# Linear attention's queries and keys: the high and the low activations in one 512-column product

## The chip, the cores and the metric

The kernel runs on one core of a Trainium2 chip. The metric is the device time of one execution in microseconds; before the change the median of three runs is 917.91 us (917.15 to 918.28). A core has a matrix engine (TensorE, in the profile PE, with its weight loads as PEld), a vector engine (VectorE, DVE), a scalar engine (ScalarE, ACT), GpSimd (POOL) and SyncE (SP), which issues most of the loads. They run side by side, each with its own queue of instructions in a fixed order, and meet at semaphores. Matrix products are accumulated in PSUM, which the kernel uses as eight banks of 128 partitions x 512 floats.

## The reference

A two-layer encoder trunk for 256 tokens of width 1024, all in float32. Of each layer, this is what the change touches:

```python
u = rms_norm(h, g_mix_pre)
(gq, gk, gv, gg, ra_f, ra_b, aq, ak, av, gate_a, gate_b) = jnp.split(u @ w_in, offsets, axis=-1)
qh = gq.astype(f32).reshape(b, s, GLA_HEADS, GLA_DK) * (GLA_DK ** -0.5)
kh = gk.astype(f32).reshape(b, s, GLA_HEADS, GLA_DK)
```

`gq` and `gk` are the queries and keys of the gated linear attention: 4 heads of 128, so 512 columns each. The other columns of the same product go to the linear attention's values, gates and decays, to the grouped-query attention (8 query heads, 2 key and value heads) and to the two branch gates. After the two branches come their merge, an output projection, a SwiGLU feed-forward part and a per-layer input embedding.

## The kernel before

**Precision in three products.** A matrix product in full float32 precision is put together from products of a faster 32-bit type. Each operand x is split into a high part (a rounding of x) and a low part (x minus the high part), and instead of x·y three products are accumulated: high·high, high·low and low·high. Weights arrive by DMA as raw float32 in units of 512 rows x 512 columns (1 MB); ACT copies a unit to its high part `wh`, DVE subtracts to get the low part `wl` (`split`, L131 to L133), in two pieces of 128x1024. The stream of units (`Stream`) runs ahead of the products by a set depth. Activations are turned by PE, so that the width lies on the partitions, and are split in the same way.

**Where the split activations lie.** `Split` (L404) keeps them in tiles of four blocks of 128 rows: `t[p, k, s, t]`, with k the block, s = 0 for high and 1 for low, and t the token (256). The high and the low part of one block of rows are therefore 512 neighbouring floats on each partition.

**The stage that is changed.** Most of the input projection uses the activations as the stationary operand and streams 512 columns of weights (`amode`). The linear attention's queries and keys are wanted turned, with the head's width on the partitions, so there the weights are stationary and the 256 tokens stream past (`wmode`, L630, called by `project_t`, L729). `project_t` works through two units of weights (halves of the 1024 rows); in each, for each of four column blocks f of 128 (a head), it issues for four blocks of rows k the products wh·high and wh·low, and after those wl·high: twelve products of 256 columns. Two heads share one bank, so a projection holds two banks. The stage at L1269 to L1280 calls it for the queries and then for the keys and empties each bank with one ACT copy of 128x512, the queries scaled by 128 to the power -0.5.

**What sets the order around it.** The program writes down the products of one stage after the other; side jobs (`Task`) are woken by a count of steps (`tick`, one per column block in `wmode`) and put their instructions between. During this stage these are the turning of the grouped-query attention's queries (L1240) and keys (L1178, split at L1180 by way of L133), its scores (L1199 by way of L105), the softmax (L1201 to L1219) and the turning of its result (L1227); right after it the linear attention's decays begin (L1296 and following), which first read the stored queries and keys in L1323 and L1324. A planner then fixes each engine's order ahead of the run from its own estimate of durations and from priorities (the order of writing, moved ahead in places), and gives out the PSUM banks. At run time each engine follows its list.

Of the kernel before, what the change touches and what calls it, by code (L numbers as in the profile page):

```python
# [13 lines left out]
AF = mybir.ActivationFunctionType  # L14
ALU = mybir.AluOpType
AX = mybir.AxisListType

P = 128
T = 256
# [40 lines left out]
def trunk_kernel(ctx: ExitStack, tc: tile.TileContext, a: dict, out: bass.AP):  # L60
# [7 lines left out]
    nc = tc.nc  # L68
# [13 lines left out]
    def nm(s):  # L82
        uid[0] += 1
        return f"{s}_{part[0]}_{uid[0]}"

    def big(dt=F32):
        return bigp.tile([P, 2048], dt, tag="big", name=nm("big"))
# [4 lines left out]
    def acc():  # L92
        return accp.tile([P, 512], F32, tag="acc", name=nm("acc"))

    def aux():
        return accp.tile([P, 512], F32, tag="acc", name=nm("aux"))

    def t512():
        return smp.tile([P, 512], F32, tag="t512", name=nm("t512"), bufs=5)
# [4 lines left out]
    def mm(o, lhsT, rhs, start, stop):  # L104
        return nc.tensor.matmul(o, lhsT, rhs, start=start, stop=stop)  # L105
# [7 lines left out]
    def passes(o, parts, start, stop, fresh=False, between=None, **kw):  # L113

        ps = [((xh, yh), (xh, yl), (xl, yh)) if fresh else ((xh, yh), (xl, yh), (xh, yl)) for (xh, xl), (yh, yl) in parts]
        seq = [p for t in ps for p in t[:2]] + [t[2] for t in ps]
        for n, (x, y) in enumerate(seq):  # L120
            nc.tensor.matmul(o, x, y, start=start and n == 0, stop=stop and n == len(seq) - 1, **kw)  # L121
            if between is not None and 2 * (n + 1) == len(seq):
                between()

    def vmul(out, in0, in1):
        nc.vector.tensor_tensor(out=out, in0=in0, in1=in1, op=ALU.mult)
# [9 lines left out]
    h = cp.tile([P, 2, D], F32, tag="h", name="h")  # L136
# [30 lines left out]
    def unit(w, kh, c0):  # L167

        return lambda t: [
            (  # L170
                t[:, :2048].rearrange("p (k c) -> p k c", c=512),
                w[kh * 512 : (kh + 1) * 512, c0 : c0 + 512].rearrange("(k p) c -> p k c", p=P),
            )
        ]
# [29 lines left out]
    for l in range(DEPTH):  # L204
# [6 lines left out]
        pair = [unit(w, kh, C_GB + j * 512) for kh in range(2) for j in range(2)]  # L211
# [12 lines left out]
        for x in FFN.replace("p", ""):  # L224
            if x == "1":
                pair = pairs.pop(0)
# [170 lines left out]
    def tick():  # L397

        for t in list(tasks):
            t.left -= 1  # L400
            if t.left <= 0:
                t.go()

    class Split:  # L404
# [33 lines left out]
        def all(self, k):  # L438
            return [t[:, 0, :] for t in self.at(k, 1, 0, T)]

    def transpose_in(sp, src, k, n, hf, plain=None):

        ps = aux()
        for i in range(n):
            nc.tensor.transpose(ps[:, i * P : (i + 1) * P], src[:, i * P : (i + 1) * P], ident)
        with tc.high_priority(AHEAD):
            sp.put(ps[:, : n * P], k, n, hf * P, P)
        if plain is not None:
            nc.scalar.copy(plain, ps[:, : n * P])
# [68 lines left out]
    def turn_in(sp, x, hf, wait, plain=None, apart=False):  # L518


        def turn():
            yield wait
            for j, y in enumerate(halves(x)):
                if j and apart:
                    yield 1
                transpose_in(sp, y, 4 * j, 4, hf, plain and plain[j])

        sp.makers[hf].append(Task(turn(), part[0]))
# [100 lines left out]

    def wmode(os_, sp, k0, w, first, last):  # L630

        wh, wl = (t[:, :2048].rearrange("p (k c) -> p k c", c=512) for t in w)
        for hf in range(2):
            sp.need(hf, k0)
        for f in range(4):  # L640
            o = os_[f // 2][:, (f % 2) * T : (f % 2 + 1) * T]
            s = slice(f * P, (f + 1) * P)
            parts = [((wh[:, k, s], wl[:, k, s]), sp.all(k0 + k)) for k in range(4)]
            passes(o, parts, first and f % 2 == 0, last and f % 2 == 1, True)
            tick()

    def times(o, act, first=True, then=None):
# [38 lines left out]
    def seven(sp, forms, gated, alone=()):  # L686

        made, task = forms
        quad = lambda hf, j: lambda k: sp.tok(4 * j + k, hf)
        form = lambda i: lambda k: [p[:, k, :] for p in made[i]]  # L690

        def add(out, x, y):
            nc.vector.tensor_tensor(out=out, in0=x, in1=y, op=ALU.add)

        (p1, v), (p3, p7) = (halves(mid()) for _ in range(2))
        c11, p5, o = acc(), acc(), []
        c12, c22 = p3, p7

        def product(i, then):

            o[:] = [acc()]
            times(o[0], form(i), True, then)

        def both():
            add(v, o[0], v)
            add(c12, v, p3)
            add(c22, v, p7)

        def last():
            vsub(v, p5, c22)  # L710
            gated(1, v, c22)

        times(c11, quad(0, 0), True, lambda: nc.scalar.copy(p1, c11))
        yield
        task.need()
        product(0, lambda: nc.scalar.copy(p3, o[0]))
        yield
        times(p5, form(1), True, lambda: vsub(v, p5, p1))
        yield
        product(2, lambda: nc.scalar.copy(p7, o[0]))  # L720
        yield
        product(3, both)
        yield
        times(c11, quad(0, 1), False, lambda: gated(0, c11, c12))
        yield
        times(p5, (lambda k: [x[:, k * P : (k + 1) * P] for x in alone]) if alone else quad(1, 1), False, last)
        yield

    def project_t(sp):  # L729

        o = [acc(), acc()]
        for kh in range(2):
            wmode(o, sp, kh * 4, ws.take(), kh == 0, kh == 1)
            ws.done()
        return o

    def project(sp):

        o = [acc(), acc()]
        for kh in range(2):  # L740
            w = ws.take()
            for hf in range(2):
                amode(o[hf], sp, hf, kh * 4, w, kh == 0, kh == 1)
            ws.done()
        return o
# [80 lines left out]
    uT = Split()  # L826
# [195 lines left out]
    for l in range(DEPTH):  # L1022
# [109 lines left out]
        o = {}  # L1132
# [137 lines left out]
        ws.depth = 3  # L1270
        qk = big().rearrange("p (x h t) -> p x h t", x=2, t=T)
        for x in range(2):
            o = project_t(uT)
            for i in range(2):
                dst = qk[:, x, 2 * i : 2 * i + 2, :]
                src = o[i].rearrange("p (h t) -> p h t", t=T)
                if x == 0:
                    nc.scalar.activation(dst, src, AF.Copy, bias=0.0, scale=P**-0.5)
                else:
                    nc.scalar.copy(dst, src)  # L1280


        part[0] = f"{l}gla"
# [137 lines left out]
        for j in range(2):  # L1421
            o = project(uT)
            for hf in range(2):
                dst = gg[:, hf, j * 512 : (j + 1) * 512]
# [67 lines left out]
        def merge(br):  # L1492
            def then(j, hf, o):
                sl = [s[:, hf, j * 512 : (j + 1) * 512] for s in sgate[: br + 1]]
                vmul(sl[br], o, sl[br])
                if br == 1:
                    nc.vector.tensor_tensor(out=sl[0], in0=sl[0], in1=sl[1], op=ALU.add)

                    def turn():
                        yield WAIT_MIX[hf]  # L1500
                        transpose_in(mixT, sl[0], 4 * j, 4, hf)

                    mixT.makers[hf].append(Task(turn(), part[0], j))

            return then
# [44 lines left out]
        def turned(src, k, n, hf, wait=WAIT_FFN):  # L1550


            def turn():
                yield wait
                transpose_in(hid, src, k, n, hf)

            hid.makers[hf].append(Task(turn(), part[0], k // 4))

        for hf in range(2):
            ws.lend = hf == 1  # L1560
            for b in range(2):
                o = acc()
# [42 lines left out]
        def pair(b):  # L1605
            def gated(hf, gate, up):
                sg = t512()
                nc.scalar.activation(sg, gate, AF.Silu)
                vmul(sg, up, sg)
                turned(sg, 2 * b, 4, hf, WAIT_LAST[hf] if b == PAIRS[-1] else WAIT_PAIR)  # L1610

            return seven(u2, forms, gated)

        o = []
# [96 lines left out]
        uT = nxt  # L1711
# [47 lines left out]
```

## Time and profile before

| | |
|---|---|
| median of three runs | 917.91 us (917.15 to 918.28) |
| the profiled execution | 916.88 us, span of its instructions 914.8 us |
| busy share of the span | PE 99%, PEld 85%, DVE 86%, ACT 64%, POOL 11% |
| queries' and keys' projections, layer 0 | 41.4 to 70.1 us |
| queries' and keys' projections, layer 1 | 498.7 to 527.5 us |
| mean granted clock of TensorE | 0.997 of full speed |

How to read the rows that follow. In a row of the timeline stand the start in microseconds from the span's beginning, the time from the first start to the last end, the engine, the line of the kernel, the operation, the tile written, an arrow, the tiles read, the shape and the number of instructions in a row; square brackets give idle time before it and who ended it. Matmuls are pipelined, so the duration of a row of them is longer than the distance to the next row's start, and the distance is what they cost. In rows of a tile, `min/median/max` are durations of one instruction in nanoseconds. In the table by stretch, each engine has its busy time in microseconds and the number of its instructions.

### The profile page before, as it was taken

Reading aid. Unit: us, or ns where it says so; the run is one execution under the profiler, and the core shown is the slowest. Engines: PE = TensorE matmul, PEld = TensorE weight load, DVE = VectorE, ACT = ScalarE, POOL = GpSimd, SP = SyncE. Lnnn points to the kernel's source line nnn. Section 1 sums busy time; section 2 is a strip of 40 time slices with the busy share of each in tenths; the row PEclk is TensorE's granted clock in tenths of the full one; section 3 lists DMA queues with packets and bytes.
Section 4 is the critical chain, followed back from the end, with each engine's and each line's share of the span. In section 5 each row is a group of like instructions: output and inputs, shape, how many; then the busy total and the mean of one; then the engine's idle time right before and its main releaser. Section 6 shows DMA issues by size and latency. Waiting matters only on the chain.

```text
span 914.8 us, 12463 instructions
## 1 busy us (share of the span) xinstructions
PE 906.7 (99%) x4679; PEld 776.8 (85%) x4679; DVE 786.3 (86%) x1009; ACT 583.9 (64%) x971; POOL 99.9 (11%) x157
## 2 busy tenths in 40 slices
PE   9999999999999999999999999999999999999996
PEld 8998888888888888888899988888888888888886
DVE  7889989987679998999779789899876899989984
ACT  6688767465567565666676687675644766565563
POOL 3700220400100000000324001110001000000001
PEclk9999999999999999999999999999999999999998
DMA  8663445667385555657566424455573846555361
GB/s 285 213 201 121 139 140 189 214 186 255 123 297 182 197 191 205 228 169 262 176 249 231 138 92 139 138 184 184 196 253 123 277 164 215 219 172 222 134 234 47
DMA packets 89513, 173.47 MB, mean 190 GB/s; under 512 B 3486, under 2 KB 27558, under 8 KB 88940
## 3 DMA queue, kind: packets, MB, share of 16 engines
q1 hardware_dynamic: 89292, 172.53, 55.5%
q8 instruction: 37, 0.61, 0.3%
q14 instruction: 24, 0.20, 0.1%
q10 hardware_dynamic: 160, 0.14, 0.0%
HBM read 169.50 MB, written 3.15 MB: 189 GB/s over the span
## 4 chain that ended last, share of the span: by engine, by line
PE 95%; ACT 1%; DVE 1%; DMA 1%; issue 1%; POOL 0%; POOLq 0%
PE acc_1ffnin L121 12%; PE acc_0ffnin L121 12%; PE acc_1gate L121 7%; PE acc_0gate L121 7%; PE acc_1ffnin L105 7%; PE acc_0ffnin L105 7%; PE acc_0gqk L121 3%; PE acc_1gqk L121 3%; PE acc_0wout L121 2%; PE acc_1wout L121 2%; PE acc_1gg L121 2%; PE acc_0gg L121 2%; PE acc_1v L121 2%; PE acc_0v L121 2%; PE acc_1merge L121 2%; PE acc_0merge L121 2%
## 5 line engine op out<-in xcount | busy, mean ns | idle before, releaser
L133 ACT CAST wh_1ffnin<-raw_1ffnin 128x1024 fp32r<-128x1024 f32 x38 | 38.5, 1048 | 25.9 <-PE acc_1ffnin L105 10.2
L133 ACT CAST wh_0ffnin<-raw_0ffnin 128x1024 fp32r<-128x1024 f32 x38 | 38.2, 1048 | 25.1 <-PE acc_0ffnin L105 9.3
L133 DVE TENSOR_TENSOR wl_1ffnin<-raw_1ffnin,wh_1ffnin 128x1024 fp32r<-128x1024 f32 x38 | 45.0, 1221 | 7.6 <-ACT wh_1ffnin L133 7.4
L133 DVE TENSOR_TENSOR wl_0ffnin<-raw_0ffnin,wh_0ffnin 128x1024 fp32r<-128x1024 f32 x38 | 44.7, 1220 | 7.2 <-ACT wh_0ffnin L133 7.2
L105 PE MATMUL acc_1ffnin<-wh_1ffnin,big_1ffnin 128*128 128x512 f32 x176 | 45.1, 390 | 0.0
L105 PE MATMUL acc_0ffnin<-wh_0ffnin,big_0ffnin 128*128 128x512 f32 x176 | 45.1, 390 | 0.0
L121 PE MATMUL acc_1ffnin<-wh_1ffnin,big_1wout 128*128 128x512 f32 x168 | 42.5, 393 | 0.0
L121 PE MATMUL acc_0ffnin<-wh_0ffnin,big_0wout 128*128 128x512 f32 x168 | 42.5, 393 | 0.0
L105 PEld LDWEIGHTS acc_1ffnin<-wh_1ffnin,big_1ffnin 128*128 128x128 f32 x176 | 33.0, 188 | 6.9
L105 PEld LDWEIGHTS acc_0ffnin<-wh_0ffnin,big_0ffnin 128*128 128x128 f32 x176 | 33.0, 188 | 6.9
L133 DVE TENSOR_TENSOR wl_0ffnin<-lent_0ffnin,wh_0ffnin 128x1024 fp32r<-128x1024 f32 x30 | 35.8, 1218 | 2.2 <-ACT wh_0ffnin L133 2.2
L133 DVE TENSOR_TENSOR wl_1ffnin<-lent_1ffnin,wh_1ffnin 128x1024 fp32r<-128x1024 f32 x30 | 35.8, 1218 | 1.9 <-ACT wh_1ffnin L133 1.9
L121 PEld LDWEIGHTS acc_1ffnin<-wh_1ffnin,big_1wout 128*128 128x128 f32 x168 | 31.1, 188 | 6.2
L121 PEld LDWEIGHTS acc_0ffnin<-wh_0ffnin,big_0wout 128*128 128x128 f32 x168 | 31.1, 188 | 6.2
L133 ACT CAST wh_0ffnin<-lent_0ffnin 128x1024 fp32r<-128x1024 f32 x30 | 30.7, 1052 | 8.2 <-PE acc_0ffnin L105 3.9
L133 ACT CAST wh_1ffnin<-lent_1ffnin 128x1024 fp32r<-128x1024 f32 x30 | 30.7, 1052 | 7.5 <-PE acc_1ffnin L105 3.9
L133 ACT CAST wh_0gate<-raw_0gate 128x1024 fp32r<-128x1024 f32 x20 | 20.0, 1049 | 15.6 <-DMA raw_0gate<-in_w_o_attn_dram 6.5
L133 DVE TENSOR_TENSOR wl_0gate<-raw_0gate,wh_0gate 128x1024 fp32r<-128x1024 f32 x20 | 24.0, 1244 | 6.5 <-ACT wh_0gate L133 6.4
L133 ACT CAST wh_1gate<-raw_1gate 128x1024 fp32r<-128x1024 f32 x20 | 19.9, 1048 | 14.1 <-DMA raw_1gate<-in_w_o_attn_dram 6.3
L133 DVE TENSOR_TENSOR wl_1gate<-raw_1gate,wh_1gate 128x1024 fp32r<-128x1024 f32 x20 | 23.5, 1221 | 5.4 <-ACT wh_1gate L133 5.3
L105 PE MATMUL acc_0ffnin<-wl_0ffnin,big_0ffnin 128*128 128x512 f32 x88 | 24.6, 394 | 0.0
L105 PE MATMUL acc_1ffnin<-wl_1ffnin,big_1ffnin 128*128 128x512 f32 x88 | 24.6, 394 | 0.0
(724 smaller groups left out, 2711.3 us busy)
## 6 DMA issues: line engine op xcount, KB each, us to landing
raw_0ffnin<-in_w_ffn_out_dram SPq DMA_DIRECT2D x11, 1024.0 KB, 5.9
raw_1ffnin<-in_w_ffn_out_dram SPq DMA_DIRECT2D x11, 1024.0 KB, 5.4
lent_0ffnin<-in_w_ffn_in_dram SPq DMA_DIRECT2D x6, 1024.0 KB, 7.5
lent_1ffnin<-in_w_ffn_in_dram SPq DMA_DIRECT2D x6, 1024.0 KB, 7.8
raw_0v<-in_w_in_dram SPq DMA_DIRECT2D x4, 1024.0 KB, 5.1
raw_0gate<-in_w_o_gla_dram SPq DMA_DIRECT2D x4, 1024.0 KB, 5.9
raw_0gate<-in_w_o_attn_dram SPq DMA_DIRECT2D x4, 1024.0 KB, 5.2
raw_0wout<-in_w_ffn_in_dram SPq DMA_DIRECT2D x8, 512.0 KB, 4.7
```

Of the source, the lines that this page charges most:

```text
L105: return nc.tensor.matmul(o, lhsT, rhs, start=start, stop=stop)
L121: nc.tensor.matmul(o, x, y, start=start and n == 0, stop=stop and n == len(seq) - 1, **kw)
L133: return nc.scalar.copy(hi, src), nc.vector.tensor_tensor(out=lo, in0=src, in1=hi.bitcast(F32), op=ALU.subtract)
```

## The change

`wmode` gets four banks instead of two, one for each column block. For each block of rows the stationary high weights meet high and low activations in one product of 512 columns: the high tokens' result lands in the first half of the bank and the low tokens' in the second half. The products with the low weights stay 256 columns wide and are added onto the first half. So eight products of 256 columns become four of 512, and four of 256 stay. The sum of the two halves is made when a bank is emptied: ACT copies the first half (scaled, for the queries) to the stored queries or keys, and DVE reads the second half, scales it and adds it to them. The number of steps that wake side jobs is the same.

```diff
+        def pair(self, k):
+            return self.t[k // 4][:, k % 4, :, :]
...
         wh, wl = (t[:, :2048].rearrange("p (k c) -> p k c", c=512) for t in w)
         for hf in range(2):
             sp.need(hf, k0)
-        for f in range(4):
-            o = os_[f // 2][:, (f % 2) * T : (f % 2 + 1) * T]
+        for f, o in enumerate(os_):
             s = slice(f * P, (f + 1) * P)
-            parts = [((wh[:, k, s], wl[:, k, s]), sp.all(k0 + k)) for k in range(4)]
-            passes(o, parts, first and f % 2 == 0, last and f % 2 == 1, True)
+            for k in range(4):
+                mm(o, wh[:, k, s], sp.pair(k0 + k), first and k == 0, False)
+            for k in range(4):
+                mm(o[:, 0:T], wl[:, k, s], sp.all(k0 + k)[0], False, last and k == 3)
             tick()
...
     def project_t(sp):
 
-        o = [acc(), acc()]
+        o = [acc() for _ in range(4)]
...
         for x in range(2):
-            o = project_t(uT)
-            for i in range(2):
-                dst = qk[:, x, 2 * i : 2 * i + 2, :]
-                src = o[i].rearrange("p (h t) -> p h t", t=T)
-                if x == 0:
-                    nc.scalar.activation(dst, src, AF.Copy, bias=0.0, scale=P**-0.5)
-                else:
-                    nc.scalar.copy(dst, src)
+            for i, o in enumerate(project_t(uT)):
+                dst, r = qk[:, x, i, :], 1.0 if x else P**-0.5
+                nc.scalar.activation(dst, o[:, 0:T], AF.Copy, bias=0.0, scale=r)
+                nc.vector.scalar_tensor_tensor(out=dst, in0=o[:, T:], scalar=r, in1=dst, op0=ALU.mult, op1=ALU.add)
```

## The prediction

> **What bounds the kernel.** First the page's shares, then the chain that ended last, then who waited for whom on PE.
>
> ```profile
> span 914.8 us, 12463 instructions
> PE 906.7 (99%) x4679; PEld 776.8 (85%) x4679; DVE 786.3 (86%) x1009; ACT 583.9 (64%) x971; POOL 99.9 (11%) x157
> PE 95%; ACT 1%; DVE 1%; DMA 1%; issue 1%; POOL 0%; POOLq 0%
> ```
> ```profile
> engine line waited for: us in total, times, longest us
> PE warm L105 <- POOL seed L142: 1.0, 1, 1.0
> PE acc_1rq L121 <- DVE big_0ple L133: 0.2, 1, 0.2
> ```
>
> PE is busy for 99% of the span, makes up 95% of the last chain, and the list of its waits has 1.2 us in it. So the kernel is a queue of matmuls: what leaves PE's queue comes off the end, as long as nothing else makes PE wait. DVE at 86% has little room as a mean, so I look at it in the stretches that the change touches: layer 0's two query and key products, what follows them, and the same two in layer 1.
>
> ```profile
> core 0: us, PE busy (x) PEld busy (x) DVE busy (x) ACT busy (x) POOL busy (x), PEclk, DMA share, GB/s
> 41.40:54.40 13.00, 13.00 (x111) 12.96 (x111) 10.98 (x18) 10.78 (x25) 3.67 (x5) 1.00 0.61 190
> 54.40:70.10 15.70, 15.70 (x134) 15.70 (x133) 14.03 (x30) 12.76 (x28) 0.00 (x0) 1.00 0.72 242
> 70.10:92.00 21.90, 21.90 (x111) 18.45 (x110) 20.01 (x31) 18.80 (x40) 0.00 (x0) 1.00 0.30 99
> 498.70:513.20 14.50, 14.50 (x122) 14.35 (x121) 11.35 (x23) 7.98 (x16) 1.40 (x3) 1.00 0.72 245
> 513.20:527.50 14.30, 14.30 (x122) 14.30 (x122) 10.54 (x22) 10.84 (x26) 0.00 (x0) 1.00 0.27 79
> ```
>
> PE has no gap in any of the five. The granted clock is 1.00. DVE is free for 2.0, 1.7, 1.9, 3.1 and 3.8 us.
>
> **Matmuls: what goes.** The groups that write acc_0gqk, and who empties it (layer 1 has the same counts):
>
> ```profile
> L121 PE MATMUL acc_0gqk<-big_start,wh_0rq x64: 277/283/364, 41.5 to 53.9; 128*128 128x256 f32 x64
> L121 PE MATMUL acc_0gqk<-big_start,wl_0rq x32: 280/283/286, 42.4 to 54.4; 128*128 128x256 f32 x32
> L1278 ACT ACTIVATE big_0gqk<-acc_0gqk x2: 599/600/600, 50.9 to 54.7; 128x512 f32<-128x512 f32 x2
> L1280 ACT COPY big_0gqk<-acc_0gqk x2: 585/596/607, 68.1 to 69.8; 128x512 f32<-128x512 f32 x2
> ```
>
> Per projection 64 products with the high weights wh and 32 with the low ones wl, all 256 columns wide. With four projections (queries and keys, two layers) the 256 wh products become 128 of 512 columns; the 128 wl products stay as they are. The durations above overlap one another (pipelining), so a product's price is the distance from start to start:
>
> ```profile
> 37.83 1.07 PE L121 MATMUL acc_0kv<-wl_0rq,big_start 128*128 128x512 f32 x4
> 38.74 1.98 PE L121 MATMUL acc_0kv<-wh_0rq,big_start 128*128 128x512 f32 x8
> 40.56 1.07 PE L121 MATMUL acc_0kv<-wl_0rq,big_start 128*128 128x512 f32 x4
> 41.46 1.12 PE L121 MATMUL acc_0gqk<-big_start,wh_0rq 128*128 128x256 f32 x8
> 42.41 0.64 PE L121 MATMUL acc_0gqk<-big_start,wl_0rq 128*128 128x256 f32 x4
> 42.90 1.12 PE L121 MATMUL acc_0gqk<-big_start,wh_0rq 128*128 128x256 f32 x8
> ```
>
> Sixteen products of 512 columns take 41.46 - 37.83 = 3.63 us, 226.9 ns each; twelve of 256 take 42.90 - 41.46 = 1.44 us, 120.0 ns each. The columns streamed are the same before and after; what goes is a fixed share per product. One merge saves 2 x 120.0 - 226.9 = 13.1 ns, and 128 merges save **1.68 us**. The weight load that goes with each is inside these distances. Activations are long there: the same ones serve the earlier products from 37.83 on, so asking for high and low at once adds no wait.
>
> **Emptying: what is added.** Eight ACT copies of 128x512 become sixteen of 128x256, and sixteen DVE operations are new: each reads the other half from the bank and adds it to ACT's result. The nearest rows, each with 128x256 from PSUM:
>
> ```profile
> 46.98 0.48 DVE L469 SCALAR_TENSOR_TENSOR big_0kv<-acc_0kv,rs_start,big_0kv 128x256 fp32r<-128x256 f32 x1
> 35.95 0.42 DVE L126 TENSOR_TENSOR mid_0rq<-acc_0rq,rope_start 128x256 f32<-128x256 f32 x1
> 47.84 0.48 ACT L468 ACTIVATE big_0kv<-acc_0kv,rs_start 128x256 fp32r<-128x256 f32 x1
> 50.32 0.37 ACT L133 CAST big_0kv<-aux_0kv 128x256 fp32r<-128x256 f32 x1
> ```
>
> DVE gains 16 x 0.42 to 0.48 = 6.7 to 7.7 us; I take 0.48, since that row is the same operation: 1.9 us per projection. ACT goes from 8 x 0.60 = 4.8 to 16 x 0.37 to 0.48 = 5.9 to 7.7 us; I take 0.48, since it is the scaled form: 0.7 us more per projection. Behind a new DVE operation, which waits for its ACT copy (a pair is 0.48 + 0.48 = 0.96 us, where one copy of 0.60 stood), DVE has weight splits queued, and PE waits for those only when they come late.
>
> None of it is on PE's path if the gaps take it. They nearly do: 1.9 us fits the first stretch (2.0 free) and both of layer 1; the second is 0.2 us over (1.7 free) and spills into the idle time right behind it:
>
> ```profile
> 69.81 1.28 DVE L133 TENSOR_TENSOR mid_0at<-aux_0at,mid_0at 128x512 fp32r<-128x512 f32 x2
> 72.98 1.29 DVE L1303 SCALAR_TENSOR_TENSOR mid_0gla<-aux_0gla,mid_0gla 128x512 f32<-128x512 f32 x2 [1.89 <-ACT mid_0gla L1302]
> 78.22 0.68 DVE L126 TENSOR_TENSOR t_0gla<-big_0gqk,t_0gla 128x512 f32<-128x512 f32 x1
> 58.50 2.36 DVE L133 TENSOR_TENSOR wl_0gqk<-raw_0kv,wh_0gqk 128x1024 fp32r<-128x1024 f32 x2
> 70.10 2.00 PE L121 MATMUL acc_0v<-wh_0gqk,big_start 128*128 128x512 f32 x8
> ```
>
> The queries and keys are first read at 78.22, 8.5 us after the last product, so their longer way costs nothing. Weights are split far ahead: the unit done at 58.50 + 2.36 = 60.86 is used at 70.10, 9 us later, so a split pushed back by 1.9 us is still in time, and so is the next load that takes its raw buffer. Without that cover the whole 7.7 us of DVE would come on top: the far end for this term. No row excludes a small gain either, since the order of instructions is drawn up anew: the lower end is the 0.2 us wait of the list and two more like it, 0.6 us less. I take 0, with the rows of margin as the reason.
>
> **Banks.** A projection now holds four PSUM banks of eight where it held two. The fullest moment is in layer 0:
>
> ```profile
> 58.59 1.12 PE L121 MATMUL acc_0gqk<-big_start,wh_0kv 128*128 128x256 f32 x8
> 60.03 1.60 PE L105 MATMUL aux_0at<-big_0kv,mid_0at 128*128 128x256 f32 x12
> 60.38 0.56 ACT L1210 ACTIVATE mid_0at<-aux_0at,mx_0at,qss_0rq 128x256 f32<-128x256 f32 x1
> ```
>
> At 60.03 the keys' third block of columns is done (three banks), two banks of scores are being read by the exponentials until 60.94, and two new ones begin: seven. It fits, by one; I take 0.
>
> **Sum.** The profiled execution took 916.88 us around its span of 914.8, 1.03 us under the median of 917.91. 916.88 - 1.68 = 915.2 for such an execution, and 917.91 - 1.68 = **916.2** for the median: 0.18% less. Runs of before range over 917.15 to 918.28, so I take 0.2% (1.84 us) as what can be told from no change. The sum lies just inside it, and about half of its outcomes go beyond.
>
> **Rivals.**
> 1. **PE waits for the attention's keys (slower).** The scores stand right behind a DVE split of the turned keys, in the very stretches that get new DVE work:
>
> ```profile
> 53.26 2.36 DVE L133 TENSOR_TENSOR wl_0kv<-raw_0rq,wh_0kv 128x1024 fp32r<-128x1024 f32 x2 [0.53 <-ACT wh_0kv L133]
> 55.54 0.42 DVE L133 TENSOR_TENSOR big_0kv<-aux_0kv,big_0kv 128x256 fp32r<-128x256 f32 x1
> 56.19 1.36 PE L105 MATMUL aux_0at<-big_0kv,mid_0at 128*128 128x256 f32 x10
> 510.04 0.41 DVE L133 TENSOR_TENSOR big_1kv<-aux_1kv,big_1kv 128x256 fp32r<-128x256 f32 x1
> 510.21 1.77 PE L105 MATMUL aux_1at<-big_1kv,mid_1at 128*128 128x256 f32 x12
> ```
>
> Layer 0's split ends at 55.96 and PE goes on with the scores at 56.19: 0.23 us of margin. In layer 1 there is none (PE starts at 510.21, the split ends at 510.45). If the planned order puts the new operations ahead of these splits and PE's order isn't moved with them, PE stands for up to 1.9 us per layer: 917.91 - 1.68 + 3.8 = 920.0. It decides from 0.84 us per layer, two operations of 0.48. Against it: in layer 0 PE already does products between the first scores and these, so the order can give way. Chance 0.20.
> 2. **A bank comes too late.** An eviction stuck behind a pair of splits (2.36 us, as at 53.26) holds a bank that PE needs, where seven of eight are in use. Once per layer: 917.91 - 1.68 + 2 x 2.36 = 921.0. Against it: three of four banks are needed 1.4 us and more after the one before. Chance 0.06.
> 3. **The fixed share isn't saved.** If a product into two halves of a bank costs as much as two products, 2 x 120.0, the PE term is 0: 917.9, no change. The rows above speak against it, since 512 columns at 226.9 ns already fill a whole bank. The Trainium skill (TensorE: Matmul & The Clock Gate, section "Wait — 56ns, not 53.3ns?") has a fixed cost of only about 2.5 ns per warm matmul, measured on bf16. By that figure 128 merges would give an estimated 0.3 us; this trace's f32 products show 13.1 ns and disagree with it. Chance 0.04.
> 4. **A little more than the sum.** The new order also loses PE's small waits, 0.6 us: 917.91 - 1.68 - 0.6 = 915.6. Nothing in the change aims at them. Chance 0.12.
>
> **Chances.** The sum has the remaining 0.58; half goes beyond 0.2% (0.29), half stays within (0.29). Faster: 0.29 + 0.12 = 0.41. Same: 0.29 + 0.04 = 0.33. Slower: 0.20 + 0.06 = 0.26. The likeliest case alone holds 915.4 to 917.0 (the runs' spread around it). The range over all cases reaches from 915.0 (rival 4 and the same spread) to 920.0, rival 1's full price; rival 2 and half of rival 1's outcomes beyond are left out.
>
> **What would show it.** Right: 128 products of 512 columns at about 227 ns write acc_0gqk and acc_1gqk, 64 each, beside 64 each of 256 at 120; a layer's two projections take 0.84 us less; PE's list of waits stays near 1.2 us; sixteen DVE rows of about 0.48 us and sixteen ACT rows of 0.4 to 0.5 read the banks. Wrong: a wait of PE on big_0kv or big_1kv (rival 1), on a DVE operation that reads acc_0gqk or acc_1gqk (rival 2), or products at 240 ns (rival 3).

## The result and the profile after

The changed kernel takes 915.57 us (median of 22 runs, 914.70 to 917.20) against 917.40 us before (22 runs, 916.21 to 919.63): a ratio of 0.998 with a 95% interval of 0.9973 to 0.9986, so 1.8 us faster, 1.3 to 2.5 by the interval. In a later set of runs it is 915.48 against 917.10, a ratio of 0.9981 (0.9972 to 0.9990).

The page of the changed kernel's first profiled execution: its span, the engines' busy times with the number of instructions, and the DMA queue q8 (packets, MB, share), which matters below.

```profile
span 915.2 us, 12243 instructions
PE 905.9 (99%) x4551; PEld 769.6 (84%) x4551; DVE 791.1 (86%) x1025; ACT 584.5 (64%) x979; POOL 103.0 (11%) x157
...
q8 instruction: 36, 0.59, 0.3%
```

PE has 128 products fewer, DVE 16 operations and ACT 8 more: the change as written. The span is 0.4 us longer than before's, although the median is shorter. This execution took 917.14 us, at the slow end of its runs, and the list of PE's waits shows where most of that lies:

```profile
engine line waited for: us in total, times, longest us
PE warm L105 <- POOL seed L142: 1.0, 1, 1.0
PE aux_1emb L994 <- DMA mid_0ffnout<-in_p_dram: 0.6, 1, 0.6
PE acc_0rq L105 <- ACT wh_start L142: 0.5, 1, 0.5
PE acc_0ffnin L121 <- ACT wh_0emb L133: 0.2, 1, 0.2
```

The last three rows lie at loads or at the start, away from the changed stage. A second profile of the same kernel spans 913.3 us and has the first row alone. One execution is not the median, so differences are read by stage below.

The groups that write and empty layer 0's queries and keys, and the timeline of PE where they begin and end:

```profile
L105 PE MATMUL acc_0gqk<-big_start,wh_0rq x32: 387/393/477, 41.9 to 53.9; 128*128 128x512 f32 x32
L105 PE MATMUL acc_0gqk<-big_start,wl_0rq x32: 274/282/365, 42.8 to 54.5; 128*128 128x256 f32 x32
...
L1274 ACT ACTIVATE big_0gqk<-acc_0gqk x8: 387/402/411, 52.3 to 70.3; 128x256 f32<-128x256 f32 x8
L1275 DVE SCALAR_TENSOR_TENSOR big_0gqk<-acc_0gqk,big_0gqk x8: 400/410/415, 56.3 to 72.1; 128x256 f32<-128x256 f32 x8
```
```profile
41.91 1.07 PE L105 MATMUL acc_0gqk<-big_start,wh_0rq 128*128 128x512 f32 x4
42.82 0.64 PE L105 MATMUL acc_0gqk<-big_start,wl_0rq 128*128 128x256 f32 x4
43.29 1.09 PE L105 MATMUL acc_0gqk<-big_start,wh_0rq 128*128 128x512 f32 x4
44.22 0.63 PE L105 MATMUL acc_0gqk<-big_start,wl_0rq 128*128 128x256 f32 x4
44.70 1.09 PE L105 MATMUL acc_0gqk<-big_start,wh_0rq 128*128 128x512 f32 x4
...
69.93 2.00 PE L121 MATMUL acc_0v<-wh_0gqk,big_start 128*128 128x512 f32 x8
```

A column block takes 44.70 - 43.29 = 1.41 us, where it took 1.44. Layer 0's stage runs from 41.91 to 69.93, 28.02 us against 70.10 - 41.46 = 28.64. For layer 1, the same two edges on PE's timeline, of before and then of after:

```profile
498.85 0.88 PE L121 MATMUL acc_1gqk<-big_0ple,wh_1rq 128*128 128x256 f32 x6
527.65 0.63 PE L121 MATMUL acc_1v<-wh_1gqk,big_0ple 128*128 128x512 f32 x2
```
```profile
499.97 0.84 PE L105 MATMUL acc_1gqk<-big_0ple,wh_1rq 128*128 128x512 f32 x3
511.05 1.87 PE L105 MATMUL aux_1at<-big_1kv,mid_1at 128*128 128x256 f32 x12
528.27 1.09 PE L121 MATMUL acc_1v<-wh_1gqk,big_0ple 128*128 128x512 f32 x4
```

28.30 us against 28.80. Together the two stages are 1.12 us shorter, in the second profile too (28.03 and 28.29). The attention's scores at 511.05 take 1.87 us where they took 1.77: DVE hands over the turned keys 0.1 us later. The reason stands on DVE's timeline, first of before, then of after: ahead of the split of the attention's queries (mid_1at), which the keys' split follows, DVE was idle for 0.86 us, and now two of the new additions stand there.

```profile
509.44 0.69 DVE L133 TENSOR_TENSOR mid_1at<-aux_1at,mid_1at 128x512 fp32r<-128x512 f32 x1 [0.86 <-ACT mid_1at L133]
```
```profile
509.74 0.74 DVE L1275 SCALAR_TENSOR_TENSOR big_1gqk<-acc_1gqk,big_1gqk 128x256 f32<-128x256 f32 x2
510.40 0.68 DVE L133 TENSOR_TENSOR mid_1at<-aux_1at,mid_1at 128x512 fp32r<-128x512 f32 x1
```

The queries' split starts 0.77 us ahead of the scores before, and 0.65 us ahead of them after.

### The profile page after: what moved, and what is told of

Same layout as the page of the kernel before. It is cut to its first block, busy times and chain, and to the rows that moved or that the text cites. A ratio compares the mean times of both kernels' runs of the same rounds, so it can differ in the third digit from the quotient of the medians.

```text
span 915.2 us, 12243 instructions
## 1 busy us (share of the span) xinstructions
PE 905.9 (99%) x4551; PEld 769.6 (84%) x4551; DVE 791.1 (86%) x1025; ACT 584.5 (64%) x979; POOL 103.0 (11%) x157
## 4 chain that ended last, share of the span: by engine, by line
PE 90%; DVE 4%; DMA 3%; issue 1%; ACT 1%; POOL 0%; SPq 0%; POOLq 0%; ACTq 0%; DVEq 0%
PE acc_1ffnin L121 12%; PE acc_0ffnin L121 10%; PE acc_1gate L121 7%; PE acc_0gate L121 7%; PE acc_1ffnin L105 7%; PE acc_0ffnin L105 4%; PE acc_1rq L121 3%; PE acc_1gqk L105 2%; PE acc_0gqk L105 2%; PE acc_1wout L121 2%; PE acc_0gg L121 2%; PE acc_1gg L121 2%; PE acc_1v L121 2%; PE acc_0v L121 2%; PE acc_1merge L121 2%; PE acc_0merge L121 2%
```

## The experiments

Theory A: the gain is PE's merged products alone, and the work added on DVE and ACT is hidden. Theory B: the four banks, the emptying in two halves or the new plan bring it. Theory C: the additions on DVE cost something, so the merge saves more than is seen.

**The changed kernel once more.**

> The changed kernel beside the others of this set. Theory A (the gain is PE's merged products alone): 1.1 to 1.7 us under before, the two stages of queries and keys together 1.1 us shorter than before's 57.44 us, and the longer layer-0 feed-forward stretch of the first profile (179.57 us against 178.55) back at 178.6. Theory B (the new plan moved something else): that stretch stays at 179.5, and the gain comes from another stage.

Measured: 915.48 us, 1.6 under before. The two stages are 1.12 us shorter; layer 0's feed-forward stretch is 178.99 us, nearer to before's 178.55 than to the 179.57 of the first profile. Two more profiles of before have 178.77 and 178.63, and a third, of before with a longer start, has 179.55: a long one comes and goes with the execution.

**The products cut back.**

```diff
-                mm(o, wh[:, k, s], sp.pair(k0 + k), first and k == 0, False)
+                hi, lo = sp.all(k0 + k)
+                mm(o[:, 0:T], wh[:, k, s], hi, first and k == 0, False)
+                mm(o[:, T:], wh[:, k, s], lo, False, False)
```

> The change with its four banks and its emptying kept, and each product of 512 columns cut back into two of 256, one for each half of the bank. Theory A: the whole gain is gone, 0 +- 0.4 us against before, and the two stages take 57.4 us again. Theory B (banks, emptying or the new plan bring the gain): still 1 us or more under before. Theory C (the additions on DVE cost something that the merge pays for): slower than before by that cost, 0.5 us or more.

Measured: 916.88 us, ratio to before 0.9996 (0.9987 to 1.0005). The two stages take 28.64 and 28.89 us, layer 0's the same as before to the hundredth, layer 1's 0.09 us longer by its late scores. So the banks, the emptying and the sixteen additions cost nothing and bring nothing that can be told in the kernel's time; the gain goes when the merge goes, and theory B falls.

**Without the additions.**

```diff
-                nc.vector.scalar_tensor_tensor(out=dst, in0=o[:, T:], scalar=r, in1=dst, op0=ALU.mult, op1=ALU.add)
```

> The change without the sixteen additions on DVE: the products with the low activations are made and left in the bank. Theory A (the additions are hidden): as fast as the changed kernel within 0.4 us. Theory C (the additions cost): faster than it by 0.5 us or more, most of it where PE waits for the scores of layer 1.

Measured: 915.78 us, ratio to before 0.9990 (0.9981 to 0.9999), not faster than the change. Layer 0's stage is 0.55 us longer than the change's (28.58 us). Most of it lies at the end, where the first product of the values starts 0.50 us behind the product before it instead of 0.12; 0.1 us is at the scores. On ACT's and PE's timelines:

```profile
71.01 1.25 ACT L1274 ACTIVATE big_0gqk<-acc_0gqk 128x256 f32<-128x256 f32 x4
71.49 2.11 PE L121 MATMUL acc_0v<-wh_0gqk,big_start 128*128 128x512 f32 x8 [0.22 <-ACT big_0gqk L1274]
```

That product reads nothing that the copy writes; what the copy gives free is a bank. Layer 1's stage is 0.12 us shorter (28.17), with the scores on time. The order of instructions that comes with leaving the additions out thus loses something of its own, and this run alone does not settle what they cost. The kernel with the products cut back does: it has all sixteen, and takes layer 0's stage in before's time and layer 1's in 0.09 us more. They are hidden but for that tenth, and theory C falls.

**Every addition twice.**

```diff
+                nc.vector.scalar_tensor_tensor(out=t512()[:, 0:T], in0=o[:, T:], scalar=r, in1=dst, op0=ALU.mult, op1=ALU.add)
```

> The change with every addition on DVE made twice, the second into a tile that nobody reads: 16 more operations of 0.41 us, 1.6 us per projection, on top of the 1.6 us that the change added. Theory A with the free time of the profile before (2.0, 1.7, 3.1 and 3.8 us): layer 0 is over by some 1.5 us per projection, which has the idle time at 71 us and the lead of the weights left to go to; PE stands for 0 to 0.5 us, so at most 0.5 us slower than the change. Theory C (every addition is on the path): 16 x 0.41 = 6.6 us slower, or a good part of it.

Measured: 916.75 us, 1.3 us slower than the change, ratio to before 0.9996 (0.9988 to 1.0005): between the two expectations, more than A's 0.5 and far from C's 6.6. Layer 0's stage is 1.09 us longer than the change's (29.11) and the values' stage behind it 0.8 (31.83 against 31.02); layer 1's is 0.3 shorter (27.99), where another order leaves no late scores. Two rows of its list of PE's waits, the first at the end of layer 0's stage and the second in the values' stage, then PE and DVE at the end of layer 0's stage:

```profile
PE acc_0v L121 <- DVE mid_0at L133: 0.9, 1, 0.9
PE aux_0at L105 <- DVE mid_0at L133: 0.5, 1, 0.5
```
```profile
69.72 0.63 PE L105 MATMUL aux_0gla<-raT,mid_start 81*128 81x256 f32 x4
71.27 2.11 PE L121 MATMUL acc_0v<-wh_0gqk,big_start 128*128 128x512 f32 x8 [0.91 <-DVE mid_0at L133]
```
```profile
70.53 1.28 DVE L133 TENSOR_TENSOR mid_0at<-aux_0at,mid_0at 128x512 fp32r<-128x512 f32 x2
71.73 1.22 DVE L133 TENSOR_TENSOR wl_0gqk<-raw_0gqk,wh_0gqk 128x1024 fp32r<-128x1024 f32 x1
72.86 0.75 DVE L1275 SCALAR_TENSOR_TENSOR big_0gqk<-acc_0gqk,big_0gqk 128x256 f32<-128x256 f32 x2
```

The product that waits doesn't read mid_0at. What DVE's operation can give it is the PSUM bank that this operation read, while banks of the keys are still waiting to be emptied at 72.86. The kernel without the additions waits at the same product, for an ACT copy of a bank. So the cover that hides the additions is between one and two of them per bank deep, and what runs out first is a bank. That it is the bank is inferred from the tiles, not shown by a run of its own.

**The fixed share of a product.** The values' and gates' products, cut in two:

```diff
+            if cut:
+                for j in range(2):
+                    c = slice(j * 256, (j + 1) * 256)
+                    nc.tensor.matmul(o[:, c], x, y[:, c], start=start and n + j == 0, ...)
...
-        for hf, o in enumerate(project(uT)):
+        for hf, o in enumerate(project(uT, True)):
...
-            o = project(uT)
+            o = project(uT, True)
```

> The change, and beside it every 512-column product of the linear attention's values and gates (four projections a layer, 384 products in all) cut into two of 256 columns on the same bank. What a cut costs is read where the rest of the kernel is untouched. Theory A with start-to-start distances (2 x 119.7 ns for the cut, 228 to 229 for the whole one in those stages): 10.5 to 12 ns a cut, the four stages together 4.0 to 4.6 us longer, and all of it in the kernel's time: 2.2 to 2.8 us slower than before, 4.0 to 4.6 slower than the change. With the 2.5 ns that the Trainium skill gives (TensorE: Matmul & The Clock Gate, section on the 56 ns): 1.0 us slower than the change, still under before.

Measured: 920.05 us, ratio to before 1.0028 (1.0018 to 1.0039), 2.9 us over before, where the change is 1.6 under: 4.5 us apart. The gates' stage of layer 0 in the table by stretch, of the change's second profile and of this kernel:

```profile
100.50:135.44 34.94, 34.94 (x204) 30.66 (x203) 30.97 (x60) 24.19 (x51) 4.67 (x8) 1.00 0.48 157
```
```profile
102.82:138.83 36.01, 36.01 (x301) 35.75 (x299) 30.20 (x59) 24.92 (x52) 4.62 (x8) 1.00 0.47 147
```

96 cuts cost 1.07 us; the four stages together are 4.30 us longer, 11.2 ns a cut, and all of it arrives in the kernel's time. PE's queue is the bound, and a product has a fixed share. This is over four times the roughly 2.5 ns that the Trainium skill states (TensorE: Matmul & The Clock Gate, section "Wait — 56ns, not 53.3ns?").

**Why a merge saves less than a cut costs.** From start to start within the stage, a merged product takes 231.6 ns in the mean of its four places in a run of four, and a wl product 118.2, against 119.7 before.

```diff
-                mm(o[:, 0:T], wl[:, k, s], sp.all(k0 + k)[0], False, last and k == 3)
+                mm(o, wl[:, k, s], sp.pair(k0 + k), False, last and k == 3)
```

> The change with the low weights' products widened to 512 columns too (low times low is then computed as a fourth term). The stages hold no 256-column products of the projection any more. If the 231.8 ns that a merged product takes in the changed kernel come from its turns with the 256-column ones, it is 227 here; if they belong to this stage (weights stationary, high and low tokens streaming), it stays at 232. The kernel is 128 x (232 - 118) = 14.6 us slower than the change, or 128 x (227 - 118) = 14.0 us.

Measured: one run, 930.14 us, 13.0 over its set's before and so 14.6 over the change. PE's timeline at the start of its layer-0 stage:

```profile
42.22 1.07 PE L105 MATMUL acc_0gqk<-big_start,wh_0rq 128*128 128x512 f32 x4
43.13 1.07 PE L105 MATMUL acc_0gqk<-big_start,wl_0rq 128*128 128x512 f32 x4
44.03 1.07 PE L105 MATMUL acc_0gqk<-big_start,wh_0rq 128*128 128x512 f32 x4
44.94 1.07 PE L105 MATMUL acc_0gqk<-big_start,wl_0rq 128*128 128x512 f32 x4
45.85 0.39 PE L105 MATMUL acc_0gqk<-big_start,wh_0rq 128*128 128x512 f32 x1
```

Sixteen in 45.85 - 42.22 = 3.63 us, 226.9 ns each; over both stages 228.2 in the mean, 227 at the median. With nothing but wide products the 231.6 are gone, so they belong to the turns with the narrow ones, not to this stage. What in the turns costs it stays open. The two stages together are 13.44 us longer than the change's, near the forecast of 14.0 for 227 ns; the other 1.2 us of this one execution lies elsewhere in the kernel and was not traced.

**The rest of the gain.** The two stages give 1.12 us of 1.8. Going through all stages of before and after, two more differ. The one in which layer 1's values are made is 0.13 us shorter in the mean (31.17, then 31.01 and 31.07), and 31.03 in the kernel with the products cut back, so this small part comes with the banks and the emptying that it keeps. The step from layer 1's first product to its keys took 24.76 us in before and takes 24.33, though the change doesn't touch it. Two more looks at before:

> The kernel before once more, for a second profile. If its stage from the end of the embedding to layer 1's first keys (24.76 us in the first profile, 24.33 in the changed kernel's) is a property of its plan, it is 24.76 again, with PE's 0.3 us step near 473 us; if it is chance of the loads, it comes out at 24.33.

> The same for a third profile: 24.76 us again by the plan, anything between 24.33 and 25.2 by chance. The two stages of queries and keys stay at 28.64 and 28.80 us in either case.

Measured: 25.43 and 24.32 us: neither a property of the plan alone nor the same chance for both kernels, since every kernel with the merged products has 24.32 or 24.33. In the long executions PE waits for split activations (0.8 us in the second look, 0.2 in the first profile). DVE and ACT have the same order there, but run late behind one cast of weights on ACT. Its row on ACT's timeline in before, and in the changed kernel's second profile:

```profile
463.57 2.06 ACT L133 CAST wh_0ple<-raw_0ple 128x1056 fp32r<-128x1056 f32 x2 [1.24 <-DMA raw_0ple<-in_w_in_dram]
```
```profile
461.90 2.05 ACT L133 CAST wh_0ple<-raw_0ple 128x1056 fp32r<-128x1056 f32 x2
```

Layer 1's first product starts at 462.89 and 462.50, so the cast is 0.68 us behind it in before and 0.60 us ahead of it after. It waits for a load. In the DMA view of the 2 us up to that product, before has one transfer of queue q8, and the changed kernel has none:

```profile
q8 instruction: 1, 0.02, 2.9%
```

Every packet of this queue has 16384 bytes. The page counts 37 of them for before's 2 x 4679 products and weight loads, 36 for 2 x 4551 after, and 39 for 2 x 4935 with the values and gates cut: these are the blocks in which PE's program comes in, some 253 of the counted instructions each. Layer 0's change takes out 64 products and 64 loads, half a block, and moves all later fetches by as much. (A block of 8192 bytes on queue q14 comes 1.7 to 2.2 us ahead of that product in every one of the twelve profiles, so it makes no difference.) Theory D: a fetch that falls on the tail of this load delays it. Theory E: the merged products, or their plan, do. To tell them apart, both kernels get half a block of idle products at the start:

```diff
     warm_up(WARM[1], True)
+    warm_up(64)
```

> The kernel before with 64 idle products (128x128 on constants) added to PE's warming up at the start, which lengthens PE's program by 128 instructions, half of one of the 16384-byte blocks in which it is fetched. The start is some 4 to 7 us later for it; read is only the step from layer 1's first product to its keys. Theory D (a block fetched at the tail of a weight load delays it): the fetch that stood 0.8 to 2.0 us ahead of that first product is gone from there, the cast of that load starts 0.5 to 0.8 us ahead of the product as in the changed kernel (before: 0.2 to 1.4 us behind it), and the step takes 24.33 us. Theory E (the merged products themselves, or the plan): the cast stays 0.2 to 1.4 us behind, the step is 24.3 to 25.4 us.

> The changed kernel with the same 64 idle products at the start. Theory D: a fetch stands again 0.8 to 2.0 us ahead of layer 1's first product, the cast starts 0.2 to 1.4 us behind it, and the step takes 24.3 to 25.4 us as in the profiles before. Theory E: no change, the cast 0.5 to 0.8 us ahead and 24.33 us.

Measured, with all profiles; times are from layer 1's first product, worked out from the DMA records and the rows of ACT and PE. "None" means no fetch from 8 us ahead to 7.5 us behind. The four single executions took 917.91 and 918.93 us (the two looks at before), 921.43 (before, shifted) and 919.99 (change, shifted); single times are not compared here.

| kernel | fetch starts | cast starts | step to the keys, us |
|---|---|---|---|
| before, three profiles | -1.37, -0.83, -2.01 | 0.68, 1.36, 0.17 | 24.76, 25.43, 24.32 |
| products cut back | -1.46 | 1.06 | 25.14 |
| change, two profiles | none | -0.56, -0.61 | 24.33, 24.33 |
| without additions / additions twice | none | -0.77 / -0.54 | 24.33 / 24.32 |
| four terms | none | -0.62 | 24.33 |
| values and gates cut | -2.60 | -0.02 | 24.33 |
| before, shifted | none | -0.65 | 24.33 |
| change, shifted | -2.44 | 0.02 | 24.33 |

The two shifted kernels' casts:

```profile
466.84 2.06 ACT L133 CAST wh_0ple<-raw_0ple 128x1056 fp32r<-128x1056 f32 x2
```
```profile
466.78 2.06 ACT L133 CAST wh_0ple<-raw_0ple 128x1056 fp32r<-128x1056 f32 x2 [0.61 <-DMA raw_0ple<-in_w_in_dram]
```

Shifting takes the fetch away from the kernel before, and its cast is early; it brings one back to the changed kernel, and its cast waits for the load again, 0.6 us later than without. So theory D holds for the load, and theory E, which has before's cast late and the change's early whatever the shift, falls. With a fetch every cast is later than any without, and by and large a later fetch means a later cast (-1.46 and -1.37 are out of order).

How the load is delayed stands in the records of its landing. In all twelve executions it is issued 6.63 to 6.66 us ahead of the product, and it lands in sixteen parts. Without a fetch the last part is in 0.84 to 1.27 us ahead of the product. In each of the six executions with one, a single part comes 1.1 to 1.6 us after the end of the fetch, at -0.04 to 1.34, while all others are in by -1.1 (with the products cut back one more comes at -0.48). So what the fetch holds up is one part in sixteen, and the cast waits for all of them.

The step follows the cast: starts of 0.68, 1.06 and 1.36 us cost 0.43, 0.81 and 1.10 us, that is, what lies beyond 0.25 us, and 0.17 costs nothing. That PE stands for it was seen in three of the four profiles whose fetch lies between -2.01 and -0.83, and in none with an earlier fetch: the shifted change came out at -2.44, ahead of the forecast -2.0 to -0.8, its cast at 0.02, short of the forecast 0.2 to 1.4, and it lost nothing on PE. The shifts thus take away and bring back the cast's delay; a cost on PE they did not bring back. By the profiles the step is worth (24.76 + 25.43 + 24.32) / 3 - 24.33 = 0.5 us in the mean, from three executions. The kernel with the products cut back has before's 4679 products again, and so this fetch as well: its time takes back both the merge's saving and the fetch's. Theory A's "alone" holds for the two stages only; the 0.5 us comes of the merge too, but by way of the program's length.

## Why the prediction came out right

- **Sum and direction.** Forecast 916.2 us and 1.68 less; measured 915.57 and 1.83 less (1.62 in the later set). The two agree partly by luck: the stages give 1.12, layer 1's values 0.13, the fetch 0.5 in the mean, together 1.75. A layer's two projections were to take 0.84 us less; they take 0.62 and 0.50 less.
- **Matmuls (mis-sized).** 1.68 us was forecast from 226.9 and 120.0 ns. The products now take 231.6 and 118.2 ns: a column block goes from 12 x 119.7 = 1436 ns to 4 x 231.6 + 4 x 118.2 = 1399, and 32 blocks save 1.19 us (layer 0's stage, where PE has no wait, gives 0.62 for its 16 blocks). The prices were read from stretches of one width; in alternation the wide product loses most of 5 ns against them. The scores of layer 1 take back 0.1: the prediction had the added work at nothing on PE's path, and the two additions ahead of the split cost that much.
- **Emptying.** Sixteen DVE rows of 0.41 to 0.42 us at the median (0.48 was taken) and sixteen on ACT of 0.39 to 0.40 (0.48 was taken) are hidden, as said, but for the 0.1 us at layer 1's scores: cutting the products back gives before's time. The spill of the second stretch into the idle time behind it is there, on DVE's timeline of the changed kernel: three additions from 71.48 on, and 0.69 us idle behind them where 1.89 stood.

```profile
71.48 1.08 DVE L1275 SCALAR_TENSOR_TENSOR big_0gqk<-acc_0gqk,big_0gqk 128x256 f32<-128x256 f32 x3
73.25 1.29 DVE L1298 SCALAR_TENSOR_TENSOR mid_0gla<-aux_0gla,mid_0gla 128x512 f32<-128x512 f32 x2 [0.69 <-ACT mid_0gla L1297]
```

- **Banks.** No wait in the change. With the additions doubled it is the end of this stage, and not the fullest moment at 60 us, where PE stands.
- **Rival 1** shows in miniature: 0.1 us at layer 1's scores, none in layer 0, against a full price of 1.9 each. Even the 0.1 is not always paid: with the same additions layer 1's stage takes 28.17 us in the profiles of the shifted change and of the kernel with the values and gates cut. **Rival 2** needs twice the additions. **Rival 3** falls with the cuts at 11.2 ns. **Rival 4** (small waits of PE vanish) is what happened beside the sum, by a way that the prediction didn't name: the position of PE's program blocks against a load.

## What to carry to other kernels

Where one matrix engine's queue is the whole path, a product's fixed share (11 ns here) times the products saved goes nearly whole off the end (a merge brought 9 ns here), but read the price from a stretch that has the same mix of widths. Find out how deep the cover for the added work is by doubling that work: here once was all but free and twice cost 1.3 us. When a stage that a change doesn't touch gets faster or slower, compare where the program's own blocks are fetched before believing in the plan.

## What was not expected of the hardware

A fetch of one 16384-byte block of PE's program, in flight for 0.93 to 1.04 us, is enough to delay one of the sixteen parts of a 1 MB weight load whose tail it meets, so that its first user starts 0.6 to 2 us later than without it. In a kernel with 99% of PE busy this was worth up to 1.1 us of the end (25.43 against 24.33), and 64 idle products at the far start of the program were enough to move it away or back.
